# A hybrid decoder block on one core: VectorE's S5 parameters as two interleaved chains, the skip term as a matrix product, and the gates' steps in groups

## The chip, the core and the metric

The kernel runs on one core of a Trainium2 chip. The metric is the device time of one execution in microseconds. The kernel before has a median of 1624.55 us over three runs (1624.2 to 1626.63). The profiled execution took 1620.8 us, of which the trace covers a span of 1618.7 us.

## The reference

The block mixes the sequence (512 tokens, 1024 channels), retrieves experts and adds a gated embedding. Only the mixer's front matters here:

```python
z = rmsnorm(h) @ w_in                    # xs (512), u (512), v (512)
# S5: 32 groups of 16 channels, 64 complex states each
dt = exp(log_dt); mag = exp(lam_re * dt); ang = lam_im * dt
abar = mag * (cos(ang) + 1j * sin(ang))  # discretised transition
coef = (abar - 1) / (lam_re + 1j * lam_im)
bbar = coef * b                          # per group 64 x 16, complex
h[t] = abar * h[t-1] + bbar @ u[t]       # a scan over 512 positions
y = Re(c @ h) + d * u                    # d * u is the skip term
ys = gelu(y); ys = ys * sigmoid(ys @ glu_w + glu_b)      # the gates
yg = gelu(u) * (tril(ws) @ layernorm(gelu(v)) + bs)      # in chunks of 128
h = h + concat(rmsnorm(ys), rmsnorm(yg)) @ w_out
# then PEER: queries, top-k of product keys, gathered experts; a gated embedding; a last norm
```

## The kernel before, in words

The whole program is one function, and the order in which it issues work is the order on every engine's queue: nothing is rescheduled. Each engine works through its own queue in order and waits where an operand is not ready. V is VectorE, S is ScalarE, G is GpSimd (POOL in the profile), PE is TensorE, and loads and stores go through SyncE's queue.

**S5 parameters.** Sixteen pairs of groups stand on 128 partitions, so a parameter is a 128x16 tile (`pt16`). VectorE computes them by polynomials, one small step after another: `exp16` of log_dt (`dt`), then `ldt` and `exp16` again (`mag`), then `ang`, its reduction, sine and cosine (`e1c`, `e1s`), then the powers 1 to 4 of the transition (`pwr`, `pwi`), `rho`, and the coefficients (`co_re`, `co_im`). GpSimd negates `c_pad[:, 1]` into `nci`, copies the powers into `prr` and `pri`, and makes `skip`, which is the identity's last 32 columns times d.

**Blocks of four positions.** Time is cut in 128 steps of L = 4 positions. The 16 pairs are taken in four groups g of four. For each g there are:

- `s5_r(g)`: 12 VectorE products that make the input matrices `rr`, `ri`.
- `s5_par(g)`: TensorE products `ptt` (the kernel within a block of four), transposes of `rr` and `ri` (ScalarE copies them to `w4`).
- `s5_par2(g)`: VectorE adds `skip` to a part of `ptt` in PSUM (L460), then ScalarE copies `ptt` into the triangular `t4` (L461, L464).
- `u4_copy(f)`, `u4_scale(f)`: ScalarE copies of one block of `pz` into `u4` (L530), and VectorE's scaling of it by `x4` (L534).
- `s5_pv(g)`: TensorE products `pv` of `w4` and `u4`; `s5_scan(g)`: VectorE rotates them by tables `rc`, `rs` and scans; `s5_back(g)` rotates back.
- `s5_q(g)`: six VectorE products that make the output matrices `qr`, `nqi`.
- `s5_out(g)`: TensorE products `py`, and ScalarE's GELU into `ysT` (L515).

**Tables.** `rc` and `rs` are 128x16x128 tables of cosines and sines. `table_steps` doubles them seven times on VectorE: six products and sums (`cmul`, L547), and a squaring of nine small steps (`csquare`) between two doublings. It is a generator that is advanced at set places.

**The projections.** `z_mm(cc)` is the xs part of w_in (TensorE, L523, accumulated over four chunks in the four PSUM tiles `pz`). `filler` is a generator of further TensorE work: eight tiles `pj` of the embedding's projection, then v, then u. `fill(n)` advances it by n pieces. A `pj` tile takes one of the four buffers of the pool `psa`, which `pz` holds before.

**The gates.** `ys_split` splits `ysT` into two parts for the products with glu_w; `glu_mm(fo)` makes `pg`; `glu_mix(fo)` applies the sigmoid (`sg`, L709), multiplies (L710), splits the result into `mixh`, `mixl` (L170, L171) and squares it (L714). `norm_v` and `norm_v2` are the statistics and the normalisation of v on VectorE, `wo_split` splits a chunk of w_out on ScalarE and VectorE. Then come `prs` (TensorE, sums of squares, L767), `rss` (L769), `mix_v` (`pm`, L719) and the output projection `po`, whose first product follows the last `pm`.

Of the kernel before, what the change touches and what calls it, by code (L numbers as in the profile page):

```python
# [105 lines left out]
def tile_hybrid_block(ctx: ExitStack, tc: tile.TileContext, x, p_t, cols_d, rows_d, w_in, s5_b, s5_c, glu_w, ws_t,  # L106
# [14 lines left out]
    def col(name, j=0, n=1):  # L121
        o, _ = COLS[name]
        return cols[:, o + j:o + j + n]
# [149 lines left out]


    pq = [P, NPAIR]
    W = V
# [39 lines left out]
    lam_re, lam_im = col("a_re", 0, 16), col("a_im", 0, 16)  # L316
    dt = exp16(col("log_dt", 0, 16), "dt")
    ldt = pt16()
    g_tt(ldt, lam_re, dt, ALU.mult)
    mag = exp16(ldt, "mag")  # L320
    ang = pt16()
    g_tt(ang, lam_im, dt, ALU.mult)
# [24 lines left out]
    cmul(W, e1c, e1s, qc, qs, cr, sr, t1)  # L347


    pwr = sp.tile([P, NPAIR, L], F32, name="pwr")  # L350
# [38 lines left out]
    g_tt(co_im, co_im, den, ALU.mult)  # L389
    nci = sp.tile([P, NPAIR, 32], F32, name="nci")  # L390
    G.tensor_scalar(nci, c_pad[:, 1], -1.0, None, op0=ALU.mult)
    prr, pri = (sp.tile([P, NPAIR, L - 1], F32, name=f"pr{z}") for z in "ri")
# [6 lines left out]
    rhos = sp.tile([P, NPAIR, NJ], F32, name="rhos")  # L399
    rc = sp.tile([P, NPAIR, NJ], F32, name="rc")  # L400
    rs = sp.tile([P, NPAIR, NJ], F32, name="rs")
    G.memset(rc[:, :, 0:1], 1.0)
    G.memset(rs[:, :, 0:1], 0.0)
    for h in range(NF):
# [6 lines left out]
    def s5_r(g, e):  # L411
        g4 = slice(4 * g, 4 * g + 4)
        rr, ri = (fw.tile([P, 4, L, 32], F32, name=f"rr{z}", bufs=2) for z in "ri")
        t3 = fw.tile([P, 4, L - 1, 32], F32, name="t3", bufs=1)
        one = lambda a: a[:, g4, None].to_broadcast([P, 4, 32])
        cmul(e, rr[:, :, 3, :], ri[:, :, 3, :], one(co_re), one(co_im), b_pad[:, 0, g4, :], b_pad[:, 1, g4, :],
             t3[:, :, 0, :])
        shp = [P, 4, L - 1, 32]
        cmul(e, rr[:, :, 0:3, :], ri[:, :, 0:3, :], prr[:, g4, :, None].to_broadcast(shp),
             pri[:, g4, :, None].to_broadcast(shp), rr[:, :, 3:4, :].to_broadcast(shp),  # L420
             ri[:, :, 3:4, :].to_broadcast(shp), t3)
        RR[g] = rr, ri

    def s5_q(g):
        g4 = slice(4 * g, 4 * g + 4)
        qr, nqi = (fw.tile([P, 4, L, 32], F32, name=f"q{z}") for z in "ri")
        tq = fw.tile([P, 4, L, 32], F32, name="tq", bufs=1)
        a_r, a_i = (a[:, g4, :, None].to_broadcast([P, 4, L, 32]) for a in (pwr, pwi))
        c_r, c_i = (a[:, g4, None, :].to_broadcast([P, 4, L, 32]) for a in (c_pad[:, 0], nci))
        V.tensor_tensor(tq, a_i, c_i, op=ALU.mult)  # L430
        V.tensor_tensor(qr, a_r, c_r, op=ALU.mult)
        V.tensor_tensor(qr, qr, tq, op=ALU.add)
        V.tensor_tensor(tq, a_i, c_r, op=ALU.mult)
        V.tensor_tensor(nqi, a_r, c_i, op=ALU.mult)
        V.tensor_tensor(nqi, nqi, tq, op=ALU.subtract)
        QQ[g] = qr, nqi

    def s5_par(g):
# [5 lines left out]
        for q in range(4):  # L444
            o = ptt[:, q * 32:(q + 1) * 32]
            PE.matmul(o, flat(rr[:, q]), c_pad[:, 0, 4 * g + q, :], start=True, stop=False)
            PE.matmul(o, flat(ri[:, q]), nci[:, 4 * g + q, :], start=False, stop=True)
        w4 = [fw.tile([P, 4, P], F32, name=f"w4{z}") for z in "ri"]
        for z, src in enumerate((rr, ri)):
# [3 lines left out]
            S.copy(w4[z].rearrange("p a b -> p (a b)"), pw4)  # L453
        WW[g], TT[g] = w4, (t4, ptt)

    def s5_par2(g):
        t4, ptt = TT[g]
        k3 = ptt[:, 0:P].rearrange("p (q c) -> p q c", q=4)
        k0 = k3[(L - 1) * 32:]
        V.tensor_tensor(k0, k0, skip[(L - 1) * 32:, 4 * g:4 * g + 4, :], op=ALU.add)  # L460
        S.copy(t4[:, :, 3, :], k3)  # L461
        for t in range(3):
            for b in range(t + 1):
                S.copy(t4[32 * b:32 * b + 32, :, t, :], k3[32 * (b + 3 - t):32 * (b + 4 - t)])  # L464
        TT[g] = t4

# [69 lines left out]

    def table_steps():
        sq = csquare(csquare((e1c, e1s)))
        n = 1
        while n < NJ:  # L540
            tt = fw.tile([P, 3 * 4 * NJ], F32, name="tt", tag="sc", bufs=1)[:, 0:NPAIR * NJ // 2].rearrange(
                "p (a j) -> p a j", a=NPAIR)
            ei, er = (a[:, :, None].to_broadcast([P, NPAIR, n]) for a in (sq[1], sq[0]))
            o_re, o_im, b_re, b_im, t_ = rc[:, :, n:2 * n], rs[:, :, n:2 * n], rc[:, :, 0:n], rs[:, :, 0:n], tt[:, :, 0:n]
            for o, a, b, op in ((t_, b_im, ei, ALU.mult), (o_re, b_re, er, ALU.mult), (o_re, o_re, t_, ALU.subtract),
                                (t_, b_im, er, ALU.mult), (o_im, b_re, ei, ALU.mult), (o_im, o_im, t_, ALU.add)):
                V.tensor_tensor(o, a, b, op=op)  # L547
                if 2 * n == NJ:
                    yield
            n *= 2  # L550
            if n in (16, 64):
                yield
            if n < NJ:
                sq = csquare(sq)


    pjd = dpool.tile([NT, P, D], F32, name="pjd")
# [50 lines left out]
    z_mm(0)  # L608
    s5_r(0, V)
    z_mm(1)  # L610
# [5 lines left out]
    G.memset(rhos[:, :, 0:1], 0.0)  # L616
    s5_r(1, V)
    s5_par(0)
    z_mm(2)
    s5_par(1)  # L620
    tab = table_steps()
    next(tab)
    s5_par2(0)
    next(tab)
    s5_par2(1)
    z_mm(3)
    u4_copy(0)
    for n in range(4):
        next(tab)
    u4_scale(0)  # L630
    for n in range(3):
        next(tab, None)
    fill(2)
# [9 lines left out]
    s5_par(2)  # L643
    s5_par2(2)
    u4_scale(2)
# [5 lines left out]
    u4_scale(3)  # L651
    s5_q(0)
    fill(13)
# [10 lines left out]
    s5_back(1, "V")  # L664
    s5_par2(3)
    s5_q(1)
# [39 lines left out]

    def glu_mix(fo, pg):
        sg = rp_.tile([P, T], F32, name="sg", bufs=2)
        S.activation(sg, pg, AF.Sigmoid, bias=col("glu_b", fo))  # L709
        V.tensor_tensor(ysT[fo], ysT[fo], sg, op=ALU.mult)  # L710
        hi, lo = (rp_.tile([P, T], F32R, name=f"mix{z}{fo}") for z in "hl")
        split_scaled(hi, lo, ysT[fo], col("on_ssm", fo))
        mixs.append((hi, lo))
        S.activation(ysT[fo], ysT[fo], AF.Square)  # L714
# [24 lines left out]
    fill(12)  # L739
    for f in range(3):  # L740
        ys_split(f)
    norm_v2(0, *nv[0])
    nv.append(norm_v(1))
    ys_split(3)
    wo_split(0)
    wo_split(1)
    norm_v2(1, *nv[1])
    nv.append(norm_v(2))
    pgs = [glu_mm(fo) for fo in range(NF)]
    fill(8)  # L750
    for fo in range(2):
        glu_mix(fo, pgs[fo])
    norm_v2(2, *nv[2])
    nv.append(norm_v(3))
    for fo in range(2, NF):
        glu_mix(fo, pgs[fo])
    fill(100)
# [635 lines left out]
```

## Time and profile before

| | before |
|---|---|
| median of three runs | 1624.55 us |
| profiled execution | 1620.8 us |
| its span | 1618.7 us |
| mean granted TensorE clock | 0.978 |
| TensorE busy | 1533.8 us (95%) |
| VectorE busy | 1337.1 us (83%) |
| ScalarE busy | 700.5 us (43%) |
| GpSimd busy | 788.9 us (49%) |

The front, which is all that the change touches, ends at about 257 us of the span. The rest is the PEER part. A row of the timeline reads: start, duration, engine, line, operation, output and inputs, count, and in brackets the idle time of that engine ahead of it with what ended it. A row of the chain of waits reads: start, duration, what.

### The profile page before, as it was taken

The numbers are of one execution on the slowest core, as the hardware profiler recorded it, in microseconds if no ns is written. First come the engines' busy times: TensorE is split into PE (matmuls) and PEld (weight loads), VectorE is DVE, ScalarE is ACT, GpSimd is POOL, SyncE is SP. The second block draws the span as 40 slices with busy tenths as digits, with TensorE's granted clock in tenths as the row PEclk, the third lists the DMA queues.
The fourth block names the chain that finished last, engine by engine and source line by source line (L and its number), as shares of the span: only waits on it lengthen the run. The fifth ranks groups of instructions, "written<-read, shape, count | busy, mean of one in ns | idle before, by whom it ended". The sixth has DMA issues, their size and how long they took to land.

```text
span 1618.7 us, 22140 instructions
## 1 busy us (share of the span) xinstructions
PE 1533.8 (95%) x7779; PEld 1334.0 (82%) x7779; DVE 1337.1 (83%) x2688; ACT 700.5 (43%) x1262; POOL 788.9 (49%) x656
## 2 busy tenths in 40 slices
PE   7699698999999898999999999999999999999997
PEld 4355486889998898898888888888888888888886
DVE  8977453789999777769899998998899989989774
ACT  3546323333334888853333333333333333333354
POOL 2000123447887888955455554555545555545201
PEclk9899899999999999999999999999999999999999
DMA  6121113223443454588899998989898999998851
GB/s 242 46 85 52 52 39 130 89 74 115 132 144 109 148 211 186 205 313 314 298 324 332 332 342 307 340 305 349 303 351 303 339 310 330 337 316 328 289 166 66
DMA packets 124431, 366.34 MB, mean 226 GB/s; under 512 B 8736, under 2 KB 60320, under 8 KB 106272
## 3 DMA queue, kind: packets, MB, share of 16 engines
q1 hardware_dynamic: 105888, 230.70, 41.6%
q0 software_dynamic: 18432, 134.23, 22.4%
q8 instruction: 61, 1.00, 0.2%
q14 instruction: 50, 0.41, 0.1%
HBM read 331.47 MB, written 33.42 MB: 225 GB/s over the span
## 4 chain that ended last, share of the span: by engine, by line
PE 60%; DVE 18%; ACT 7%; POOL 5%; issue 5%; DMA 4%; SPq 0%; POOLq 0%; DVEq 0%; ACTq 0%
PE yp L154 9%; PE yp L155 8%; PE yp L153 8%; PE pq L155 7%; PE pq L153 7%; PE pq L154 7%; ACT stg L1095 3%; DMA g<-in_uv,idx 3%; POOL ul L167 3%; PE pgm L1094 2%; PE pz L577 1%; DVE oh L967 1%; DVE oh L964 1%; POOL g L1118 1%; PE pg L154 1%
## 5 line engine op out<-in xcount | busy, mean ns | idle before, releaser
L167 POOL TENSOR_TENSOR ul<-ust,uh 128x256 fp32r<-128x256 f32 (+1 forms) x342 | 430.1, 1284 | 186.2 <-ACT uh L160 186.0
L153 PE MATMUL pq<-hnh,uh 128*128 128x384 f32 (+1 forms) x1152 | 396.7, 344 | 0.8 <-DVE hnl L171 0.8
L155 PE MATMUL pq<-hnh,ul 128*128 128x384 f32 (+1 forms) x1152 | 394.6, 343 | 1.9 <-POOL ul L167 1.9
L154 PE MATMUL pq<-hnl,uh 128*128 128x384 f32 (+1 forms) x1152 | 393.4, 341 | 0.0
L1118 POOL DMA_INDIRECT g<-in_uv,idx x128 | 210.7, 1646 | 314.5 <-DVE y L1161 293.4
L154 PE MATMUL yp<-vl,ah 128*128 128x512 f32 x768 | 301.4, 392 | 4.0 <-DVE vl L162 4.0
L155 PE MATMUL yp<-vh,al 128*128 128x512 f32 x768 | 300.4, 391 | 0.0
L153 PE MATMUL yp<-vh,ah 128*128 128x512 f32 x768 | 298.9, 389 | 0.0
L882 ACT ACTIVATE gab<-pq 128x384 f32<-128x384 f32 x118 | 58.1, 492 | 481.7 <-PE pq L155 481.7
L153 PEld LDWEIGHTS pq<-hnh,uh 128*128 128x128 f32 x1152 | 217.2, 189 | 8.5 <-DVE hnl L171 1.0
L155 PEld LDWEIGHTS pq<-hnh,ul 128*128 128x128 f32 x1152 | 216.6, 188 | 8.9 <-POOL ul L167 3.2
L154 PEld LDWEIGHTS pq<-hnl,uh 128*128 128x128 f32 x1152 | 217.1, 188 | 7.8 <-DVE hnl L171 0.2
L162 DVE TENSOR_TENSOR vl<-vst,vh 128x1024 fp32r<-128x1024 f32 x128 | 161.9, 1265 | 21.9 <-ACT vh L160 21.7
L1150 DVE SCALAR_TENSOR_TENSOR g<-g,hrow 128x1024 f32<-128x1024 f32 x128 | 162.9, 1276 | 20.0 <-DMA g<-in_uv,idx 19.9
L154 PEld LDWEIGHTS yp<-vl,ah 128*128 128x128 f32 x768 | 144.1, 188 | 36.3 <-DVE vl L162 8.0
L155 PEld LDWEIGHTS yp<-vh,al 128*128 128x128 f32 x768 | 144.1, 188 | 29.9
L153 PEld LDWEIGHTS yp<-vh,ah 128*128 128x128 f32 x768 | 144.2, 188 | 28.4
L1161 DVE SCALAR_TENSOR_TENSOR y<-g,act,y 128x1024 f32<-128x1024 f32 x127 | 163.2, 1285 | 4.5
L1154 DVE TENSOR_TENSOR act<-act,gate 128x1 f32<-128x1 f32 (+1 forms) x117 | 156.6, 1338 | 0.0
L160 ACT CAST uh<-ust 128x1024 fp32r<-128x1024 f32 x144 | 150.9, 1048 | 0.1
L160 ACT CAST vh<-vst 128x1024 fp32r<-128x1024 f32 x128 | 134.2, 1049 | 1.2 <-DMA vst<-in_uv 1.0
L1077 POOL TENSOR_SCALAR o1P<-iota,tr 128x128 f32<-128x128 f32 x96 | 112.0, 1178 | 3.6 <-ACT tr L1034 3.6
(412 smaller groups left out, 2117.4 us busy)
## 6 DMA issues: line engine op xcount, KB each, us to landing
ust<-in_ut SPq DMA_DIRECT2D x128, 512.0 KB, 7.5
vst<-in_uv SPq DMA_DIRECT2D x128, 512.0 KB, 6.3
gd<-stg SPq DMA_DIRECT2D x12, 2048.0 KB, 7.2
gread<-gd SPq DMA_DIRECT2D x31, 768.0 KB, 8.3
ust<-in_wq SPq DMA_DIRECT2D x16, 512.0 KB, 3.4
wstage<-in_w_in SPq DMA_DIRECT2D x12, 512.0 KB, 7.8
wstage<-in_w_out SPq DMA_DIRECT2D x8, 512.0 KB, 3.5
ust<-in_ple_wg SPq DMA_DIRECT2D x8, 512.0 KB, 6.9
```

The costliest lines, as they stand in the source:

```text
L153: PE.matmul(o, lh, rh, start=start, stop=False)
L154: PE.matmul(o, lh, rl, start=False, stop=False)
L155: PE.matmul(o, ll, rh, start=False, stop=stop)
L160: S.copy(hi, src)
L162: V.tensor_tensor(lo, src, hi.bitcast(F32), op=ALU.subtract)
L167: G.tensor_tensor(l[:, sl], s[:, sl], h[:, sl], op=ALU.subtract)
L882: S.activation(ga[n], p_[:, 0:TD], AF.Gelu)
L1077: (V if e == "V" else G).tensor_scalar(o1[a], iota, i1, g, op0=ALU.is_equal, op1=ALU.mult)
L1118: G.indirect_dma_start(out=gt, out_offset=None, in_=uv, in_offset=bass.IndirectOffsetOnAxis(ap=idx[:, r:r + 1], axis=0))
L1150: V.scalar_tensor_tensor(GS[k][:, 0:D], GS[k][:, 0:D], 1.0, hrow0, op0=ALU.mult, op1=ALU.mult, accum_out=dots[:, k:k + 1])
L1154: V.tensor_tensor(act[:, k:k + n], act[:, k:k + n], gates[0][:, k:k + n], op=ALU.mult)
L1161: V.scalar_tensor_tensor(y0, t[:, D:], act[:, k:k + 1], y0, op0=ALU.mult, op1=ALU.add)
```

## The change

- A class `Later` collects VectorE's instructions instead of issuing them, and `play(a, b)` issues one of the list a, then one of the list b, until a is empty. The chain of `ldt` and `mag` goes into list `ca`, that of `ang` to `e1c`, `e1s` into `cb`; they are issued in turns. Then the powers and coefficients go into `ca` and the whole table (`tables`) into `cb`, again in turns.
- `s5_r(0)`, `s5_r(1)` and `s5_q(0)` go into `ca` and are issued in turns with further table steps; `s5_q(0)` stood behind `u4_scale(3)` before. What is left of the table is issued behind `z_mm(3)`, with `u4_scale(0)` ahead of its last two steps.
- The skip term is a third product into `ptt` (`ident` times `skip`), so that VectorE's addition in `s5_par2` goes; the ScalarE copies into `t4` are issued at the end of `s5_par`.
- `nci` is no tile of its own: `c_pad[:, 1]` is negated in place. The tile `t3` gets two buffers.
- `ys_split` of all four follows `norm_v2(0)` and `norm_v(1)`; `fill(8)`, which stood ahead of the first `glu_mix`, goes, and its pieces are issued by `fill(100)` behind the last one.
- `glu_mix` is cut in two: `glu_gate` (sigmoid and product) for all four, then `norm_v(3)`, then `glu_mix` (split and square) for all four. `sg` gets three buffers.

```diff
+    class Later:
+        def __init__(self):
+            self.ops = []
+        def __getattr__(self, name):
+            return lambda *a, **k: self.ops.append((name, a, k))
+        def play(self, n):
+            for name, a, k in self.ops[:n]:
+                getattr(V, name)(*a, **k)
+            del self.ops[:n]
+
+    def play(a, b, upto=0):
+        while len(a.ops) > upto:
+            a.play(1)
+            b.play(1)
...
     dt = exp16(col("log_dt", 0, 16), "dt")
+    ca, cb = Later(), Later()
+    W = ca
     ldt = pt16()
     g_tt(ldt, lam_re, dt, ALU.mult)
     mag = exp16(ldt, "mag")
+    W = cb
     ang = pt16()
...
     cmul(W, e1c, e1s, qc, qs, cr, sr, t1)
+    play(ca, cb)
+    cb.play(len(cb.ops))
+    W = ca
...
-    nci = sp.tile([P, NPAIR, 32], F32, name="nci")
-    G.tensor_scalar(nci, c_pad[:, 1], -1.0, None, op0=ALU.mult)
+    rc = sp.tile([P, NPAIR, NJ], F32, name="rc")
+    rs = sp.tile([P, NPAIR, NJ], F32, name="rs")
+    G.memset(rc[:, :, 0:1], 1.0)
+    G.memset(rs[:, :, 0:1], 0.0)
+
+    def tables(e):
+        tt = fw.tile([P, 3 * 4 * NJ], F32, name="tt", tag="sc", bufs=1)[:, 0:NPAIR * NJ // 2].rearrange(
+            "p (a j) -> p a j", a=NPAIR)
+        sq = csquare(csquare((e1c, e1s)))
+        n = 1
+        while n < NJ:
+            cmul(e, rc[:, :, n:2 * n], rs[:, :, n:2 * n], rc[:, :, 0:n], rs[:, :, 0:n],
+                 *(a[:, :, None].to_broadcast([P, NPAIR, n]) for a in sq), tt[:, :, 0:n])
+            n *= 2
+            if n < NJ:
+                sq = csquare(sq)
+
+    W = cb
+    tables(cb)
+    play(ca, cb)
+    nci = c_pad[:, 1]
+    G.tensor_scalar(nci, nci, -1.0, None, op0=ALU.mult)
...
-            PE.matmul(o, flat(ri[:, q]), nci[:, 4 * g + q, :], start=False, stop=True)
+            PE.matmul(o, flat(ri[:, q]), nci[:, 4 * g + q, :], start=False, stop=False)
+            PE.matmul(o, ident, skip[:, 4 * g + q, :], start=False, stop=True)
...
-        WW[g], TT[g] = w4, (t4, ptt)
-
-    def s5_par2(g):
-        t4, ptt = TT[g]
         k3 = ptt[:, 0:P].rearrange("p (q c) -> p q c", q=4)
-        k0 = k3[(L - 1) * 32:]
-        V.tensor_tensor(k0, k0, skip[(L - 1) * 32:, 4 * g:4 * g + 4, :], op=ALU.add)
         S.copy(t4[:, :, 3, :], k3)
...
     z_mm(0)
-    s5_r(0, V)
+    s5_r(0, ca)
+    play(ca, cb)
     z_mm(1)
...
-    s5_r(1, V)
     s5_par(0)
+    s5_r(1, ca)
+    s5_q(0, ca)
+    play(ca, cb)
     z_mm(2)
     s5_par(1)
-    tab = table_steps()
-    next(tab)
-    s5_par2(0)
-    next(tab)
-    s5_par2(1)
     z_mm(3)
     u4_copy(0)
-    for n in range(4):
-        next(tab)
+    cb.play(len(cb.ops) - 2)
     u4_scale(0)
-    for n in range(3):
-        next(tab, None)
+    cb.play(2)
     fill(2)
...
-    s5_q(0)
     fill(13)
...
-    def glu_mix(fo, pg):
-        sg = rp_.tile([P, T], F32, name="sg", bufs=2)
+    def glu_gate(fo, pg):
+        sg = rp_.tile([P, T], F32, name="sg", bufs=3)
         S.activation(sg, pg, AF.Sigmoid, bias=col("glu_b", fo))
         V.tensor_tensor(ysT[fo], ysT[fo], sg, op=ALU.mult)
+
+    def glu_mix(fo):
...
     fill(12)
-    for f in range(3):
-        ys_split(f)
     norm_v2(0, *nv[0])
     nv.append(norm_v(1))
-    ys_split(3)
-    wo_split(0)
-    wo_split(1)
+    for f in range(NF):
+        ys_split(f)
     norm_v2(1, *nv[1])
     nv.append(norm_v(2))
+    wo_split(0)
     pgs = [glu_mm(fo) for fo in range(NF)]
-    fill(8)
-    for fo in range(2):
-        glu_mix(fo, pgs[fo])
+    wo_split(1)
     norm_v2(2, *nv[2])
+    for fo in range(NF):
+        glu_gate(fo, pgs[fo])
     nv.append(norm_v(3))
-    for fo in range(2, NF):
-        glu_mix(fo, pgs[fo])
+    for fo in range(NF):
+        glu_mix(fo)
     fill(100)
```

More of the change, by code (lines that the diff above doesn't have):

```diff
@@ L399, in tile_hybrid_block @@
     rhos = sp.tile([P, NPAIR, NJ], F32, name="rhos")
[L400 to L403, printed above, removed]
     for h in range(NF):
@@ L413, in s5_r @@
         rr, ri = (fw.tile([P, 4, L, 32], F32, name=f"rr{z}", bufs=2) for z in "ri")
-        t3 = fw.tile([P, 4, L - 1, 32], F32, name="t3", bufs=1)
+        t3 = fw.tile([P, 4, L - 1, 32], F32, name="t3")
         one = lambda a: a[:, g4, None].to_broadcast([P, 4, 32])
@@ L422, in s5_r, with s5_q @@
         RR[g] = rr, ri
-    def s5_q(g):
+    def s5_q(g, V=V):
         g4 = slice(4 * g, 4 * g + 4)
@@ L464, in s5_par2 @@
                 S.copy(t4[32 * b:32 * b + 32, :, t, :], k3[32 * (b + 3 - t):32 * (b + 4 - t)])
-        TT[g] = t4
+        WW[g], TT[g] = w4, t4
     def s5_pv(g):
@@ L534, in u4_scale @@
         V.tensor_tensor(uf, uf, x4[:, None, :].to_broadcast([P, 4, NJ]), op=ALU.mult)
[L537 to L554, printed above, removed]
     pjd = dpool.tile([NT, P, D], F32, name="pjd")
@@ L643, in tile_hybrid_block @@
     s5_par(2)
-    s5_par2(2)
     u4_scale(2)
@@ L664, in tile_hybrid_block @@
     s5_back(1, "V")
-    s5_par2(3)
     s5_q(1)
```

## The prediction

> **What bounds the kernel now.** I read the times first, then the busy time of each engine by stage, then the timeline of one engine at a time in the stages that the edits touch, and last the chain of waits around the gates. The first fence is the page's first line and the busy time by stretch (PE, PEld, VectorE, ScalarE, GpSimd, then the granted clock).
>
> ```profile
> span 1618.7 us, 22140 instructions
> 49.10:61.59 12.49, 0.00 (x0) 0.00 (x1) 11.92 (x31) 5.93 (x23) 0.00 (x0) 0.68 0.13 43
> 181.30:196.78 15.48, 1.56 (x7) 1.29 (x6) 8.86 (x22) 7.17 (x12) 1.55 (x2) 0.67 0.11 34
> 260.00:1618.00 1358.00, 1322.64 (x6944) 1192.94 (x6944) 1154.72 (x2209) 589.62 (x1005) 757.17 (x584) 0.99 0.72 253
> ```
>
> From 260 us on TensorE is busy 1322.6 of 1358 us: the PEER part is bound by it, the diff doesn't touch it, and it should only begin earlier. What can be won lies ahead of it, where TensorE once stands still for 12.5 us and once works 1.6 us in 15.5. The next rows show who is late in the first of these: VectorE's front in order of time, then TensorE's and ScalarE's.
>
> ```profile
> 6.30 0.17 DVE L290 TENSOR_TENSOR s5p<-cols,dt 128x16 f32<-128x16 f32 x1
> 9.94 0.18 DVE L290 TENSOR_TENSOR mag<-eq,eni 128x16 f32<-128x16 f32 x1
> 10.03 0.17 DVE L290 TENSOR_TENSOR s5p<-cols,dt 128x16 f32<-128x16 f32 x1
> 13.50 0.81 DVE L339 SCALAR_TENSOR_TENSOR s5p<-s5p,s5p 128x16 f32<-128x16 f32 x4
> 16.48 0.18 DVE L290 TENSOR_TENSOR pwr<-mag,s5p 128x16 f32<-128x16 f32 x1
> 23.15 0.29 DVE L187 TENSOR_TENSOR t<-s5p,b_pad 128x128 f32<-128x128 f32 x1
> 28.33 0.29 DVE L187 TENSOR_TENSOR t<-s5p,b_pad 128x128 f32<-128x128 f32 x1
> 33.23 0.25 DVE L290 TENSOR_TENSOR s5p<-s5p 128x16 f32<-128x16 f32 x2
> 44.09 0.29 DVE L547 TENSOR_TENSOR rc<-rc,tt 128x128 f32<-128x128 f32 x1
> 45.27 0.32 DVE L460 TENSOR_TENSOR ptt<-ptt,skip 32x128 f32<-32x128 f32 x1
> 61.57 0.69 DVE L534 TENSOR_TENSOR u<-u,x 128x512 f32<-128x512 f32 x1
> 62.18 1.22 DVE L547 TENSOR_TENSOR rs<-rc,s5p 128x1024 f32<-128x1024 f32 x1
> 64.57 0.29 DVE L187 TENSOR_TENSOR t<-s5p,b_pad 128x128 f32<-128x128 f32 x1
> 88.86 0.68 DVE L430 TENSOR_TENSOR tq<-pwi,nci 128x512 f32<-128x512 f32 x1
> ```
>
> ```profile
> 28.44 0.38 PE L447 MATMUL ptt<-nci,rri 128*128 128x32 f32 x2 [1.41 <-POOL t L442]
> 42.04 7.03 PE L523 MATMUL pz<-xn,wstage 128*128 128x512 f32 x16
> 61.59 3.78 PE L564 MATMUL pj<-gu,ysT 128*128 128x512 f32 x4 [12.52 <-ACT u L530]
> 70.98 1.16 PE L472 MATMUL pv<-u,w4r 128*128 128x128 f32 x8 [1.20 <-DVE u L534]
> 94.69 0.38 PE L510 MATMUL py<-u,t 128*128 128x128 f32 x2
> 55.35 0.27 ACT L461 COPY t<-ptt 128x128 f32<-128x128 f32 x1 [7.79 <-DVE ptt L460]
> 57.25 4.28 ACT L530 COPY u<-pz 32x128 f32<-32x128 f32 x16
> ```
>
> TensorE's product `pj` at 61.59 needs a buffer that `pz` holds until `u4_copy(0)` has read it. That copy (57.25) stands on ScalarE behind the second copy of `ptt` (55.35), which waits 7.8 us for VectorE's addition of `skip`, and VectorE is in the middle of the table. So VectorE's chain of small steps sets the front up to the scans, and TensorE waits for it. The second gap is at the gates: first VectorE and TensorE, then the chain of waits, then what follows it.
>
> ```profile
> 156.12 1.89 DVE L162 TENSOR_TENSOR ysl<-ysT,ysh 128x512 fp32r<-128x512 f32 x3 [8.07 <-ACT ysh L160]
> 162.74 0.50 PE L154 MATMUL pg<-ysl,wglu2h 128*128 128x512 f32 x1 [1.10 <-DVE ysl L162]
> 171.71 9.60 PE L577 MATMUL pz<-wstage,xn 128*128 128x512 f32 x22
> 179.90 0.70 ACT sg L709
> 180.62 0.70 DVE ysT L710
> 181.35 0.73 ACT mixh L170
> 182.10 0.76 DVE mixl L171
> 182.89 0.63 ACT ysT L714
> 186.36 1.04 DVE gv L603 x4
> 190.44 0.59 DVE ysT L710
> 196.78 5.71 PE prs L767 x26
> 196.75 1.28 ACT L579 ACT_TABLE_LOAD   x1
> 199.20 1.04 ACT L160 CAST wo2h<-wstage 128x1024 fp32r<-128x1024 f32 x1
> 205.03 0.16 DVE L769 COPY rss<-prs 128x8 f32<-128x8 f32 x1
> 208.18 0.47 PE L153 MATMUL po<-wo0h,mixh 128*128 128x512 f32 x1
> ```
>
> There ScalarE and VectorE hand each other one tile at a time, with the sigmoid, the product, both parts of the split and the square in one string for each of four tiles, from 179.9 to 196.8 us. TensorE's `prs` waits for the last square.
>
> **The change part by part: the front.** *Two chains in turns.* A step of 128x16 that needs the one before starts about 0.21 us after it (the 19 steps from 6.30 to 10.03 take 0.20 each); one that doesn't starts 0.09 us after it (9.94 to 10.03). The `mag` chain has 19 steps and the `ang` chain 33, so each pair takes about 0.21 us: 19 pairs are 4.0 us, from 6.30 to 10.3, and the last 14 steps take what they take now, 13.7 (the second of the four at 13.50) to 16.48, 2.8 us at most. The powers start at about 12.8 instead of 16.48: 3.7 us won. Then 35 steps of powers and coefficients, now 16.48 to 23.15, run in turns with 35 table steps, each pair again 0.21: 7.4 us, with an allowance of 0.8 us for GpSimd's negation and `skip`, which touch the same memory in that stretch: `s5_r(0)` begins at about 20.9 instead of 23.15. Without the allowance it is 20.1; if pairs cost twice as much, it is later than before, which is the second rival.
>
> *`s5_r` and `s5_q(0)` in turns with 30 table steps.* `s5_r(0)` is 5.2 us (23.15 to 28.33), `s5_r(1)` 4.9 (28.33 to 33.23), `s5_q(0)` 4.0 (88.86 to the next step, six of 0.69 that overlap a little). A small step in the gap of a large dependent one costs nothing and elsewhere 0.09; I take 0.04 each, 1.2 us for 30. So `s5_r(0)` ends at 26.5, `s5_r(1)` at 31.9, `s5_q(0)` at 36.3. By then 65 of the 114 table steps are done. The other 49 lie now between 44.09 and the end of the table at 64.57: 20.5 us, less two additions of `skip` (0.7) and `u4_scale(0)` (0.6), 19.2 us. So `u4_scale(0)`, ahead of the last two steps of 1.2 each, stands at 36.3 + 16.8 = 53.1 instead of 61.57, and the table ends at 56.1 instead of 64.57: 8.5 us earlier.
>
> *The skip term on TensorE.* Four products more in each `s5_par`. A pair of records of that shape takes 0.38 us and overlaps the next, so 0.9 us a group, 1.5 at most. For the groups 0 and 1 it is on TensorE's path: `ptt` goes on with `rri` at 26.5 instead of 28.44, then what takes 13.6 us today (28.44 to 42.04) takes 15.4, and `z_mm(3)` starts at 41.9 and ends at 48.9, as now. Its first tile is ready a quarter into it, ScalarE is past its copies of `ptt` at about 44.4 because they wait for no addition, and `u4_copy(0)` (4.3 us) ends at 48.7. TensorE's `pj` then starts at 48.9 instead of 61.59. What is late next is VectorE: `s5_pv(0)` waits for `u4_scale(0)` until 53.8, and `s5_pv(1)`, behind `s5_r(2)` on VectorE, starts at about 61.9 instead of 70.98, 9.0 us earlier (a little over VectorE's 8.5, since `u4_copy(1)` is no longer late).
>
> From there to `s5_out(0)` TensorE has 23.7 us of work today (70.98 to 94.69), plus 0.9 for the third skip product, less some 0.7 of waits for late copies: 8.8 us are left. `s5_q(0)`'s 4.0 us leave VectorE at 88.86, where TensorE's `fill(13)` is the longer, so that gives nothing more. In group 3 the product hides behind VectorE's scan and the addition of 0.3 leaves VectorE's path. The front gives 9 us. Its bounds: 6 if every small step and every skip product costs its upper value, 11 if TensorE's warm stretch also shortens `fill(13)` (the 12.5 us gap had the clock at 0.68).
>
> *What moves at no cost.* The two memsets of `rc`, `rs` go ahead of the negation on GpSimd, which is idle there; without that cover the table's first product would wait for `c_pad`. Negating in place is the same instruction. ScalarE's copies into `t4` come earlier and wait only for `ptt`. `s5_q(0)` issues six VectorE products and no DMA; SyncE's queue is passed by nothing in the front.
>
> **The gates.** VectorE is idle 8.1 us ahead of `ysl` (156.12), so `norm_v2(0)` and `norm_v(1)`, 4.1 us (as from 186.36 to 190.44), now fit in that gap; the fourth `ysl` comes at once, and TensorE's 1.1 us wait at 162.74 goes. In the times of today, with the front's gain set aside, the four `pg` end at 170.6 (171.71 less 1.1). VectorE has by then nearly done what stands ahead of the gates: from 158.5 on one and a half times those 4.1 us and two `wo_split`, each a little over the 1.04 of ScalarE's part, some 9 us. Four sigmoids follow the `pg` as they come, since the u pieces' GELUs and the table's reload stand behind them now. After the last `pg`: sigmoid 0.70, product 0.70, `norm_v(3)` 1.6 (of the 4.1): 173.6. The first `mixh` is done in that time. Then four strings of `mixl` 0.76, square 0.63 and `mixh` 0.73, without sigmoid and product: 2.15 us each with the handing over, the last square at 181.5 instead of 196.7. This is 15.2 us.
>
> What is late next: `prs` at 181.5 (the u products, moved past nothing on TensorE, end at 180.2, from 171.71 + 9.60 - 1.1), but ScalarE must first reload its table and do four GELUs where two stood: 196.75 to 199.20 is 2.45, two more are 1.3, so `wo2h` is at 185.2. From `wo2h` to `rss` it is 5.8 us now (199.20 to 205.03), hence 191.1; the last `pm` waits for `rss`' buffer, and `po` follows after eight records, which is 0.9 to 1.8 us (`prs` takes 0.22 a record behind its wait, half of that warm), or 3.2 as today (205.03 to 208.18). I take 1.4, as TensorE has nothing else left by then: `po` at 192.5 instead of 208.18, 15.7 us. The bounds are 12.5 (3.2 for the last step, and a string of mixes that takes 0.35 us more each) and 17 (ScalarE not last). The last two loads of w_out keep waiting for the u products on SyncE's queue, which end 1.1 us earlier, and are wanted seven us later; a DMA is not late here.
>
> **The sum.** 9.0 + 15.7 = 24.7 us off the span of 1618.7: 1594.0, and the profiled execution 1596.1 instead of 1620.8. The median shown is 3.75 us above that execution, so 1599.8; I say 1600.
>
> **A rule against it.** Against the first part stands VectorE's pipeline. The Trainium skill, "VectorE: DVE Perf Modes", section "The DRAIN you can't avoid", says that the next operation doesn't start before the pipe has emptied and that leaving out the semaphore doesn't avoid it; by that rule two chains in turns take the sum of both, and the result is the second rival's 1611. The same section grants that an operation that isn't held starts earlier, and the trace sides with that half: the step at 10.03, which needs nothing of the one at 9.94, starts within the latter's 0.18 us.
>
> **The rivals.** *Only the front, or little of the gates, pays.* If ScalarE or VectorE find a new order at the gates that ends as late as now (the GELUs of u hold back all of w_out's splits), what is left is 9 + 1.1: 1614.5. For it: ScalarE's GELUs and the reload stand behind all four mixes. Against it: the mixes lose eight hand-overs.
>
> *Turns hide nothing.* If each small step costs its 0.21 whatever stands between, the 35 table steps come as 5.5 us ahead of `s5_r(0)` (today 33.23 on) and 30 more as 5.3 us among the large ones. Then `s5_r(0)` ends at 36, `z_mm(3)` at 58, the scans start 2.7 us later than now, and the front loses 2.5 us: 1624.5 + 2.5 - 15.7 = 1611. The rows at 9.94 and 10.03 speak against it.
>
> *Slower, by the clock.* The gaps go, and TensorE works more densely. If the clock that is granted in the PEER part, 0.99 over 1358 us, fell for that, each hundredth would cost 13.7 us; the change would come out slower from 0.97 on, and 1630 at 0.968. Against it: the low clocks stand in the gaps (0.68 and 0.67), and the dense 1358 us have 0.99.
>
> **How the numbers follow.** Both parts as worked out: 0.82, by itself 1594.5 to 1606 (front 6 to 11, gates 12.5 to 17, and a microsecond or two for the runs' own spread). Gates or front failing: 0.07 each, 1614.5 and 1611. Slower by the clock or another thing: 0.02, no change 0.02. The range goes from 1593.5 to 1611.5, so that it takes in the second rival. 0.2% (3.2 us) is about what a measurement can tell from no change. Faster 0.95, same 0.02, slower 0.03.
>
> **What would show it.** Right: small VectorE steps of the front start every 0.1 us; `s5_r(0)` starts near 21; TensorE's `pj` starts near 49 and `s5_out(0)` near 86; no VectorE additions on `ptt`; the last gate square lies 15 to 16 us closer to the end of `glu_mm`; `po` starts near 183 and the PEER part keeps its length. Wrong: pairs spaced 0.4 us apart; TensorE idle between the last u product and `po` for over 10 us; a longer PEER part, or its clock below 0.99.

## The result, and the profile after

The changed kernel takes 1597.67 us (median of four runs, 1595.83 to 1600.21) where the kernel before took 1624.38 in the same comparison: a ratio of 0.9839, interval 0.9815 to 0.9863. The profiled execution took 1596.47 us, its span is 1594.2; the prediction said 1600, 1596.1 and 1594.0. The same program in a second comparison gave 1601.79; what lies between the two is taken up with the experiments.

The page's first line of the changed kernel:

```profile
span 1594.2 us, 22196 instructions
```

Its busy time by stretch (TensorE, its weight loads, VectorE, ScalarE, GpSimd, then the granted clock and DMA), from the first gate product `pg` to `po`, and the PEER part from its first query product:

```profile
150.61:183.50 32.89, 30.16 (x137) 22.16 (x135) 21.27 (x48) 19.25 (x25) 5.44 (x5) 0.95 0.21 65
244.28:1594.20 1349.92, 1316.35 (x6913) 1187.22 (x6913) 1152.21 (x2205) 587.90 (x1003) 755.94 (x583) 0.99 0.72 253
```

The same two stretches of the kernel before:

```profile
158.74:208.18 49.44, 34.41 (x137) 25.79 (x135) 27.26 (x63) 19.49 (x25) 7.97 (x8) 0.79 0.14 43
267.56:1618.70 1351.14, 1316.94 (x6913) 1187.77 (x6913) 1151.77 (x2205) 588.09 (x1003) 756.24 (x583) 0.99 0.72 253
```

From `pg` to `po` it is 32.9 us instead of 49.4: 16.6 us. TensorE stood still for 15.0 us of the stretch and now for 2.7, and the same 137 products take 30.2 instead of 34.4 us, at a granted clock of 0.95 instead of 0.79. What lies ahead of it, here called the front, gives 8.1 us (`pg` at 150.61 instead of 158.74). The PEER part, counted from its first query product `pq` on, has 6913 products in both and is as long as before to within 1.2 us. Before, it begins at 267.56; the output projection and what follows it fill the 59 us from `po` to there.

The front in order of time. VectorE first (start, duration, line, operation):

```profile
6.20 0.26 DVE L285 TENSOR_TENSOR s5p<-cols,dt 128x16 f32<-128x16 f32 x2
6.41 0.17 DVE L285 TENSOR_SCALAR ex<-s5p 128x16 f32<-128x16 f32 x1
6.50 0.18 DVE L285 TENSOR_SCALAR s5p<-s5p 128x16 f32<-128x16 f32 x1
6.62 0.17 DVE L285 TENSOR_SCALAR en<-ex 128x16 f32<-128x16 f32 x1
9.92 0.17 DVE L285 TENSOR_TENSOR mag<-eq,eni 128x16 f32<-128x16 f32 x1
12.74 0.18 DVE L285 TENSOR_TENSOR pwr<-mag,s5p 128x16 f32<-128x16 f32 x1
14.69 0.60 DVE L285 TENSOR_TENSOR s5p<-s5p 128x16 f32<-128x16 f32 x1
17.04 1.07 DVE L285 TENSOR_TENSOR s5p<-s5p,s5p 128x16 f32<-128x16 f32 x1
21.56 0.29 DVE L285 TENSOR_TENSOR t<-s5p,b_pad 128x128 f32<-128x128 f32 x1
53.81 0.68 DVE L570 TENSOR_TENSOR u<-u,x 128x512 f32<-128x512 f32 x1
```

Then GpSimd, ScalarE and TensorE in the same stretch:

```profile
14.64 1.52 POOL L436 TENSOR_SCALAR c_pad<-c_pad 128x512 f32<-128x512 f32 x1 [2.54 <-DMA c_pad<-in_s_c]
17.04 1.03 POOL L442 TENSOR_TENSOR skip<-ident,cols 128x512 f32<-128x512 f32 x1
45.33 4.29 ACT L566 COPY u<-pz 32x128 f32<-32x128 f32 x16
31.19 8.15 PE L559 MATMUL pz<-xn,wstage 128*128 128x512 f32 x16
49.67 1.98 PE L580 MATMUL pj<-gu,ysT 128*128 128x512 f32 x4
62.43 1.16 PE L508 MATMUL pv<-u,w4r 128*128 128x128 f32 x8 [1.12 <-DVE u L570]
```

A step of one chain starts within the step of the other: `ex` at 6.41, the other chain's at 6.50, `en` at 6.62. The last step of the `mag` chain starts at 9.92, where it started at 9.94 before, and the 19th step of the other chain right behind it, at 10.02. ScalarE's copy of block 0 (45.33) no longer stands behind a copy that waits for VectorE, and the product `pj` starts at 49.67 instead of 61.59.

The gates, on ScalarE, VectorE and TensorE in turn:

```profile
154.01 0.69 ACT L718 ACTIVATE sg<-pg,cols 128x512 f32<-128x512 f32 x1 [1.22 <-PE pg L155]
162.41 0.69 ACT L718 ACTIVATE sg<-pg,cols 128x512 f32<-128x512 f32 x1 [2.11 <-PE pg L155]
166.10 0.63 ACT L725 ACTIVATE ysT<-ysT 128x512 f32<-128x512 f32 x1 [2.39 <-DVE mixl L171]
172.29 0.63 ACT L725 ACTIVATE ysT<-ysT 128x512 f32<-128x512 f32 x1 [0.82 <-DVE mixl L171]
176.52 1.06 ACT L160 CAST wo2h<-wstage 128x1024 fp32r<-128x1024 f32 x1
182.37 0.16 DVE L778 COPY rss<-prs 128x8 f32<-128x8 f32 x1
182.59 1.16 PE L730 MATMUL pm<-gv,wsm 128*128 128x128 f32 x8 [2.14 <-DVE rss L778]
183.50 0.67 PE L153 MATMUL po<-wo0h,mixh 128*128 128x512 f32 x1
```

Each sigmoid waits for nothing but its own `pg` (every 2.8 us), the last square is at 172.29 instead of 196.1, and `po` at 183.50 instead of 208.18. The last `pm` still waits 2.14 us for `rss`.

### The profile page after: what moved, and what is told of

The parts are those of the page before. It is cut to its first block, busy times and chain, and to the rows that moved or that the text cites. A ratio compares the mean times of both kernels' runs of the same rounds, so it can differ in the third digit from the quotient of the medians.

```text
span 1594.2 us, 22196 instructions
## 1 busy us (share of the span) xinstructions
PE 1533.3 (96%) x7811; PEld 1334.0 (84%) x7811; DVE 1328.4 (83%) x2684; ACT 699.9 (44%) x1262; POOL 788.9 (49%) x656
## 4 chain that ended last, share of the span: by engine, by line
PE 61%; DVE 20%; ACT 6%; POOL 5%; issue 5%; DMA 3%; POOLq 0%; DVEq 0%; ACTq 0%
PE yp L154 9%; PE yp L155 9%; PE yp L153 9%; PE pq L155 7%; PE pq L153 7%; PE pq L154 7%; ACT stg L1104 3%; DMA g<-in_uv,idx 3%; POOL ul L167 3%; PE pz L593 2%; PE pgm L1103 2%; DVE oh L976 1%; DVE oh L973 1%; PE pg L153 1%; PE pg L155 1%
```

## The experiments

Runs of one program spread by some microseconds, so the starts of marked instructions in each trace carry more than the times. All are from the timelines, in us: `r0` is the first step of `s5_r(0)`, `pv1` the first product of `s5_pv(1)`, `py` that of `s5_out(0)`, `sq` the last gate square, `pq` the first PEER product; PEER is the span's end less `pq`.

| kernel | r0 | pj | pv1 | py | pg | sq | po | pq | PEER | time, ratio (interval) |
|---|---|---|---|---|---|---|---|---|---|---|
| before | 23.15 | 61.59 | 70.98 | 94.7 | 158.7 | 196.1 | 208.2 | 267.6 | 1351.1 | |
| after | 21.56 | 49.67 | 62.43 | 87.0 | 150.6 | 172.3 | 183.5 | 244.3 | 1349.9 | 1597.67, 0.9839 (0.9815 to 0.9863) |
| after_again | 21.47 | 47.77 | 62.4 | 86.9 | 150.5 | 172.2 | 183.4 | 243.5 | 1354.6 | 1601.79, 0.9873 (0.9851 to 0.9896) |
| front_only | 21.47 | 49.5 | 62.35 | 87.0 | 150.5 | 187.9 | 200.7 | 260.4 | 1358.3 | 1613.92, 0.9937 (0.9915 to 0.996) |
| gates_only | 23.00 | 61.42 | 70.81 | 96.0 | 160.1 | 181.8 | 193.0 | 253.1 | 1353.5 | 1607.99, 0.9893 (0.9867 to 0.9919) |
| no_turns | 28.66 | 59.49 | 72.84 | 97.4 | 161.0 | 182.7 | 193.9 | 254.8 | 1353.4 | 1611.09, 0.9919 (0.9895 to 0.9944) |
| fill8_back | 21.65 | 49.7 | 62.54 | 87.1 | 150.7 | 182.2 | 194.6 | 254.2 | 1352.5 | 1610.63, 0.9919 (0.9891 to 0.9947) |
| string_gates | 21.68 | 49.7 | 62.60 | 87.2 | 150.8 | 176.5 | 188.3 | 247.6 | 1355.4 | 1605.35, 0.9872 (0.985 to 0.9895) |
| skip_vec | 21.54 | 50.84 | 63.13 | 88.3 | 152.4 | 174.0 | 185.3 | 246.2 | 1356.2 | 1604.88, 0.9881 (0.9866 to 0.9896) |
| q_late | 21.30 | 50.97 | 59.59 | 85.7 | 149.3 | 171.0 | 182.2 | 243.0 | 1349.5 | 1599.78, 0.9852 (0.9837 to 0.9868) |
| best | 21.46 | 47.79 | 59.2 | 86.5 | 150.1 | 165.7 | 181.4 | 241.1 | 1355.4 | 1598.45, 0.983 (0.9808 to 0.9853) |
| best2 | 21.55 | 49.54 | 59.3 | 86.1 | 149.7 | 165.3 | 181.1 | 240.5 | 1353.7 | 1595.81, 0.9821 (0.9799 to 0.9843) |

**The two halves apart.** *front_only* has the new front and the old gates, *gates_only* the reverse.

```diff
 front_only
...
-    wo_split(1)
+    fill(8)
+    for fo in range(2):
+        glu_mix(fo, pgs[fo])
     norm_v2(2, *nv[2])
-    for fo in range(NF):
-        glu_gate(fo, pgs[fo])
     nv.append(norm_v(3))
-    for fo in range(NF):
-        glu_mix(fo)
+    for fo in range(2, NF):
+        glu_mix(fo, pgs[fo])
```

> The changed front with the gates of before. Theory (two gains that add, one behind the other): the trace of the changed kernel has the first output product of the last group 8.1 us earlier, so the time is 1624.4 - 8.1 = 1616.3 us, span about 1610.6. Rival (the gates alone decide, the front's gain is only waited away there): 1624 us, no change.

> The changed gates with the front of before. Theory: the rest of the 24.5 us of the two spans, 16.4 us: 1608 us, span about 1602.3. Rival (the gates gain only because the front feeds them earlier): 1620 us or more.

Alone, the front brings `po` 7.5 us earlier and the gates 15.2; together they bring it 24.7, 2 us more than the sum. The times lie 9.7 and 15.6 us below the 1623.58 of the kernel before in that comparison. Expected were 1616.3 and 1608; measured are 1613.92 and 1607.99. So both parts pay, and neither needs the other; the rivals, in which one of them gives little, fall. The profiled execution of front_only was the slowest of its five (1620.92) and its span, 1618.7, is no shorter than before: its PEER part is 7.2 us longer, which hides the 7.5 us at `po`.

**The turns.** Each list is issued as a whole, so that the same instructions stand one chain behind the other.

```diff
     def play(a, b, upto=0):
-        while len(a.ops) > upto:
-            a.play(1)
-            b.play(1)
+        n = len(a.ops) - upto
+        a.play(n)
+        b.play(n)
```

> The changed kernel with the same VectorE steps at the same places, but each list issued whole, first a, then as many of b, instead of in turns. Theory (turns hide the 0.1 us that a dependent small step waits): the 35 table steps come as 5.5 us behind the coefficients and 30 more as 5.3 us among the large products, less some 2 us that turns cost anyway, and the first pair of chains loses 3.7 us; the scans start 9 to 11 us later than in the changed kernel, and the time is 1597.7 + 9 to 11, 1607 to 1609 us. Rival (a pair of lists takes the sum of both either way, and the gain of the front comes from ScalarE's copies that no longer wait for the addition of skip): within 2 us of 1597.7.

VectorE in that kernel, the end of the `mag` chain and the first product of `s5_r(0)`:

```profile
9.61 0.17 DVE L285 CAST eni<-en 128x16 int32<-128x16 f32 x1
9.82 0.17 DVE L285 TENSOR_TENSOR mag<-eq,eni 128x16 f32<-128x16 f32 x1
9.91 0.17 DVE L285 TENSOR_TENSOR s5p<-cols,dt 128x16 f32<-128x16 f32 x1
28.66 0.28 DVE L285 TENSOR_TENSOR t<-s5p,b_pad 128x128 f32<-128x128 f32 x1
```

A dependent step starts 0.21 us behind its forerunner (9.61 to 9.82), one of another chain 0.09 (9.82 to 9.91). `s5_r(0)` starts 7.1 us later than with turns, the scans and `po` 10.4 later, and by `py` the front is 2.7 us behind the kernel before. The rival, within 2 us of 1597.7, falls. So all of the front's gain hangs on the turns: with everything else in place, and above all with 35 table steps moved ahead of `s5_r(0)` and 30 more among the products behind it, the front is slower than before. What the other edits would give without turns and with the table where it stood was not run. The 10.4 us lie within the expected 9 to 11; the time, 1611.09, is 2 us above the expected 1607 to 1609, and in the profiles the PEER part is 3.5 us longer than after the change.

**What the gates gain by.** *fill8_back* puts the u pieces back ahead of the sigmoids and keeps the grouping; *string_gates* leaves them where the change puts them and has the strings of before.

```diff
 fill8_back
+    fill(8)
     for fo in range(NF):
         glu_gate(fo, pgs[fo])
 string_gates (the front of the change, the gates of before without this line)
-    fill(8)
```

> The changed kernel with the eight u pieces issued ahead of the gates again, as before. Theory (what counts at the gates is that the sigmoids no longer stand on ScalarE behind two GELUs that wait for the u products; the grouping is the smaller part): the first sigmoid starts about 8 us behind the last gate product again, the last square comes some 11 us later than in the changed kernel, 1597.7 + 9 to 12, about 1608 us. Rival (the grouping of the four gates is what gains): within 4 us of 1597.7.

> The changed front, and the gates of before (one string of steps for each tile, two tiles, then two norms, then two tiles) with only the eight u pieces taken away from ahead of them. Theory (ScalarE's GELUs ahead of the sigmoids were most of the loss): the first sigmoid starts within 2 us of the first gate product's end or when VectorE has done the norms, a tile takes 3.5 us, the last square comes some 4 us later than in the changed kernel, po starts at about 187.5 instead of 183.5, time about 1601.7 us. Rival (without the grouping nothing is won): po at 197 or later, 1611 us.

ScalarE, first in front_only (the old gates), then in fill8_back, then in string_gates:

```profile
169.73 0.69 ACT L595 ACTIVATE gu<-pz,xr 128x512 f32<-128x512 f32 x1 [1.03 <-PE pz L593]
...
171.72 0.69 ACT L718 ACTIVATE sg<-pg,cols 128x512 f32<-128x512 f32 x1
```

```profile
166.83 0.69 ACT L595 ACTIVATE gu<-pz,xr 128x512 f32<-128x512 f32 x1 [15.23 <-PE pz L593]
170.53 2.42 ACT L718 ACTIVATE sg<-pg,cols 128x512 f32<-128x512 f32 x4
```

```profile
155.56 0.69 ACT L718 ACTIVATE sg<-pg,cols 128x512 f32<-128x512 f32 x1 [2.65 <-PE pg L155]
161.71 0.72 ACT L170 ACTIVATE mixh<-ysT,cols 128x512 fp32r<-128x512 f32 x1 [5.45 <-DVE ysT L719]
176.46 0.63 ACT L723 ACTIVATE ysT<-ysT 128x512 f32<-128x512 f32 x1 [0.82 <-DVE mixl L171]
```

In fill8_back ScalarE waits 15.2 us for the u product that stands ahead of the sigmoids in its queue. After the change the first sigmoid could start at 154.0 and the last at 162.4; here all four come from 170.5 on, and `po` is 11.1 us later. Taking the pieces away from the old strings (front_only to string_gates) gives 12.3 us, and the rest of the gates' edits, what is left from string_gates to after, 4.8. In the other order it is 6.0 (front_only to fill8_back) and 11.1. So about two thirds of these 17 us are the wait in ScalarE's in-order queue, which the prediction hadn't separated. The smaller part is not the grouping alone: string_gates also has the old places of `ys_split`, `wo_split` and the two norms, and from its second square to its third (166.76 to 172.96) it takes 6.2 us where the others follow after 3.5. How much of the 4.8 is hand-overs and how much these places was not taken apart. Both theories were right in the points (`po` of string_gates 188.3 where 187.5 was expected), and both rivals fall: fill8_back isn't within 4 us of after, and string_gates has `po` long before 197. Both times are above what was expected, 1610.63 for about 1608 and 1605.35 for 1601.7, with PEER parts 2.6 and 5.5 us longer than after the change.

**The skip term on VectorE again.** The third product goes, the addition comes back, with the table's steps ahead of it.

```diff
-            PE.matmul(o, ident, skip[:, 4 * g + q, :], start=False, stop=True)
...
+        V.tensor_tensor(k0, k0, skip[(L - 1) * 32:, 4 * g:4 * g + 4, :], op=ALU.add)
```

> The changed kernel with the skip term added by VectorE again instead of a third product; for the groups 0 and 1 the additions stand in the middle of the table, 19 steps behind s5_q(0), where ptt is ready. Theory (what counts is where the addition stands, not which engine does it): VectorE has 0.7 us more ahead of u4_scale(0), TensorE 0.9 us less in each s5_par; the scans and the first output product within 1 us of the changed kernel's (62.4 and 87.0), time 1597.7 within 1 us. Rival (an addition on VectorE holds up ScalarE's copies and with them pj, as before): pj at 55 or later, 3 us or more lost.

TensorE's products of the second block in skip_vec, and VectorE's third addition:

```profile
63.13 2.08 PE L513 MATMUL pv<-u,w4r 128*128 128x128 f32 x8 [2.46 <-DVE u L575]
70.14 0.32 DVE L501 TENSOR_TENSOR ptt<-ptt,skip 32x128 f32<-32x128 f32 x1 [0.88 <-PE ptt L488]
```

A narrow miss in the points, and the clock is in it. The scans start 0.7 us later (63.13), as the 0.7 us of VectorE's additions say, and `py` 1.3 us later, not within 1. Between the two TensorE saves the third product's 0.9 us, but it loses 1.5 at the products `pv`, which take 2.08 us instead of 1.16 (those of the other half 1.68 instead of 1.06) at a granted clock of 0.53. ScalarE's copies do wait for the additions, as in the rival, and `pj` is 1.2 us later at 50.84, far from the rival's 55. So `po` is 1.8 us later in this profile, but without those 1.5 us the two forms would be about level: which one is better isn't shown. The time, 1604.88, lies 7.2 us above after's, and 6.3 of that are in the PEER part, which this edit doesn't touch. The last control below has 4.7 us of such a difference in one and the same program; whether all of the 6.3 is of that kind isn't shown either.

**`s5_q(0)` behind the scaling again.** With it out of the turns, the table is done earlier.

```diff
     s5_r(1, ca)
-    s5_q(0, ca)
     play(ca, cb)
...
     u4_scale(3)
+    s5_q(0)
     fill(13)
```

> The changed kernel with s5_q(0) back behind u4_scale(3), as before. Theory (its six products are 3.6 us of VectorE's time ahead of u4_scale(0), which TensorE waits for, while VectorE has 12.9 us of idle time behind s5_r(3)): the scans start 3.5 us earlier, at about 59, the first output product at about 84, and the time is 1597.7 - 3, about 1594.7 us. Rival (ScalarE's copies of u or TensorE's own work set these times, or the wait moves behind s5_back(0)): the first output product within 1 us of 87.0.

TensorE where the second block of scans begins in q_late, and the busy time and clock from there to 63.00:

```profile
59.59 2.07 PE L508 MATMUL pv<-u,w4r 128*128 128x128 f32 x8 [3.13 <-DVE u L570]
```

```profile
59.59:63.00 3.41, 3.41 (x17) 3.41 (x18) 3.34 (x6) 2.85 (x12) 0.00 (x0) 0.53 0.10 40
```

The scans are 2.8 us earlier, but `py` only 1.3 and `po` the same 1.3: TensorE had waited 3.13 us, and its first products then ran at a granted clock of 0.53, the eight shown in 2.07 us instead of 1.16, the next eight in 1.70 instead of 1.06. That is the 1.5 us by which the way from `pv1` to `py` is longer, 26.1 us instead of 24.6. After the change the low clock falls ahead of `pv1`, and from there to `py` the clock is 1.00. The expectation of 1594.7 was too low by 5, and the rival (`py` within 1 us of 87.0) isn't met either; 1599.78 is not to be told from after.

**Two steps on.** *best* takes q_late and gives the gates as a pipeline: three sigmoids and products, then splits (`mix_h`) and squares (`mix_s`) with the fourth gate in between, the last `norm_v` behind them. *best2* also moves two splits of w_out and the last norm's second half ahead of the last `fill`; those are the last three added lines and the three taken out below. The edit of q_late and the halves of `glu_mix` aren't shown.

```diff
-    for fo in range(NF):
+    for fo in range(3):
         glu_gate(fo, pgs[fo])
-    nv.append(norm_v(3))
-    for fo in range(NF):
-        glu_mix(fo)
+    mix_h(0)
+    mix_h(1)
+    glu_gate(3, pgs[3])
+    mix_s(0)
+    mix_h(2)
+    mix_s(1)
+    mix_h(3)
+    mix_s(2)
+    mix_s(3)
+    nv.append(norm_v(3))
+    wo_split(2)
+    norm_v2(3, *nv[3])
+    wo_split(3)
     fill(100)
...
-    wo_split(2)
-    norm_v2(3, *nv[3])
-    wo_split(3)
```

> As the run before (s5_q(0) late), and at the gates the mixes issued in a pipeline: the first two splits ahead of the fourth gate, each square one tile behind its split, norm_v(3) behind the squares. Theory (a string of split and square is 2.1 us by hand-overs, while ScalarE alone needs 1.3): the last square comes at 167 less 3, before TensorE's u products end, so that ScalarE's GELUs and wo2h come 4 us earlier; po starts about 7.5 us earlier than 183.5, and TensorE isn't cold there, which is 1.4 us; time about 1589 us, span 1585. Rival (TensorE's u products or the GELUs end as late, and nothing but the first part is won): 1594.7 us.

> This is the kernel with Wq's first block behind all of u's scaling and the gates in a pipeline, with the block means' weights and norms (the splits of Wo of 2 and 3, the third norm) moved ahead of the last fill of products, so that TensorE and VectorE have less to do between the last square and the first product with Wo. Theory (the chain from the last square over the last GELUs and Wo's casts to rss sets the first product): po at about 179.5 (183.50 after the change, 181.44 without the move), time about 1593. Rival (TensorE at half clock behind its waits, and the PEER part's low stretches, which fall anew in each execution, take what the points gain): po no earlier than 181, time within 2 us of after's.

TensorE in best2 from its first sums of squares on, in order of time, and behind it the busy time by stretch:

```profile
170.76 4.53 PE L786 MATMUL prs<-ones,ysT 128*128 128x2 f32 x32
175.15 6.17 PE L733 MATMUL pm<-gv,wsm 128*128 128x128 f32 x32
181.08 0.47 PE L153 MATMUL po<-wo0h,mixh 128*128 128x512 f32 x1
```

```profile
149.72:181.08 31.36, 31.36 (x137) 23.71 (x135) 25.88 (x56) 19.06 (x25) 8.77 (x6) 0.89 0.21 68
174.00:180.00 6.00, 6.00 (x30) 6.00 (x30) 4.67 (x6) 1.42 (x2) 3.60 (x2) 0.50 0.00 0
```

The squares end 7 us earlier than after the change and the first cast of `wo2h` is at 165.9 instead of 176.5, as the theory wants, yet `po` comes only 2.4 us earlier, at 181.1. The chain over the last square no longer sets it: `rss` is there at 175.33, 5.7 us ahead of `po`. TensorE has no gap in the whole stretch from `pg` to `po`, 31.36 of 31.36 us, but a granted clock of 0.50 from 174 to 180. So the theory of best2 (179.5) misses, and the rival's number (no earlier than 181) holds; its half clock is there too, but not behind a wait, as it had said. Once TensorE is the bound, what other engines save doesn't move `po`. best misses more clearly: `po` at 181.4 where 176 was expected, 0.8 us earlier than in q_late, and 1598.45 us where 1589 was expected, not to be told from after or from best2. Against after_again, which ran beside it, best2's runs are 6 us lower (1591.13 to 1597.08 against 1600.06 to 1604.11) and the two intervals of the ratio don't overlap; in the profiles `po` is 2.3 us earlier, `pq` 3.0 and the PEER part 0.9 shorter. Against the changed kernel's first comparison (1597.67) it is 1.9 us lower, and the intervals overlap. So best2 is ahead by 2.3 us at `po` for reasons that are shown; that its time is lower by more than that isn't.

**The changed kernel once more.** Unchanged.

> The changed kernel once more, unchanged, as the measure of what one profile differs from another by. Theory (up to the first PEER product the points belong to the kernel, behind it the low stretches belong to the execution): the points up to po within 0.5 us of the first profile (u4_scale 53.8, pv(1) 62.4, first block of y 87.0, gates 150.6, po 183.5), the PEER part anywhere from 1349 to 1358, time 1597.7 within 2. Rival (the low stretches belong to the kernel too): the PEER part within 1 us of 1349.9.

TensorE in after_again:

```profile
30.44 7.03 PE L559 MATMUL pz<-xn,wstage 128*128 128x512 f32 x16
47.77 1.99 PE L580 MATMUL pj<-gu,ysT 128*128 128x512 f32 x4
182.48 1.16 PE L730 MATMUL pm<-gv,wsm 128*128 128x128 f32 x8 [0.51 <-DVE rss L778]
```

The points that VectorE or ScalarE set repeat to 0.1 us (`pv1` 62.4, `py` 86.9, `po` 183.4); those that TensorE sets by itself move with the clock, as `pj` does by 1.9 us. The PEER part is 4.7 us longer, and with it the time 4.1 us higher, not within the expected 2: the rival, a PEER part within 1 us of the first, falls. What of the 4.7 us belongs to the execution and what to the chip isn't known, since the two comparisons may have run on different chips.

## Why the prediction was right

**The turns (front, first step): right.** Powers at 12.8 (12.74 measured); `s5_r(0)` near 20.9 came at 21.56. What was sized too small is the allowance for GpSimd, 0.8 us: two steps of VectorE took 0.60 and 1.07 us instead of 0.18, at the very times of GpSimd's negation (14.64) and `skip` (17.04), together 1.3 us longer. That is 0.5 of the 0.7 us by which `s5_r(0)` is late. The size could have been read from the kernel before, where the steps at these two operations (14.90 and 19.88 there) are as slow:

```profile
14.92 0.63 DVE L345 SCALAR_TENSOR_TENSOR s5p<-s5p,s5p 128x16 f32<-128x16 f32 x1
19.99 0.97 DVE L192 TENSOR_TENSOR pwi<-pwi,s5p 128x16 f32<-128x16 f32 x1
```

**The front's later points: 0.5 to 1 us late each, as they hang on that.** `u4_scale(0)` 53.1 predicted, 53.81 measured; `pj` 48.9 and 49.67; `s5_pv(1)` 61.9 and 62.43; `py` 86 and 87.04. From `s5_pv(1)` to `py` it is 24.61 us against 23.71 before: the skip product's 0.9 us was right (the products into `ptt` take from 66.04 to 68.64, where they took from 74.58 to 76.29), and the 0.7 us of late copies that the prediction took off didn't go: TensorE waits 0.73 us for `w4r` in both. At `pg` the front gives 8.1 us, not 9.0. The bounds, 6 to 11, hold.

**The gates: right, a little low.** Counted from the first `pg`, the prediction has the last square's end 22.8 us later, `wo2h` 26.5, `rss` 32.4, `po` 33.8; measured were 22.3, 25.9, 31.8 and 32.9. The strings take 2.06 us each (166.10 to 172.29 for three) where 2.15 was taken, and from `rss` to `po` it is 1.1 us instead of 1.4. So it is 16.6 us instead of 15.7: the front's error and this one cancel, and that the sum at `po` is 24.7 as predicted is an accident.

**The rest shifted whole: not quite.** Behind `po` the prediction moved everything by the same amount, but the first query product came 23.3 us earlier, not 24.7. From `po` to there it takes 60.8 us instead of 59.4, at a granted clock of 0.92 instead of 0.94: there is one stretch of half clock more, and it stands right behind `po`. The changed kernel there, and then the kernel before:

```profile
183.50:187.30 3.80, 3.80 (x13) 3.01 (x12) 3.80 (x6) 0.00 (x0) 2.71 (x2) 0.55 0.00 0
```

```profile
208.18:212.00 3.82, 3.82 (x20) 3.15 (x19) 3.82 (x12) 0.82 (x3) 1.01 (x3) 1.00 0.00 0
```

The kernel before has 20 products there, the change 13. This goes with the new gates and not with one execution: in the six profiles that have them as the change does (after, after_again, gates_only, no_turns, skip_vec, q_late) it is 60.1 to 61.0 us from `po` to `pq`, at 0.91 or 0.92; in the other six it is 59.3 to 59.7, at 0.94. What in the gates brings it isn't shown. A wait stands ahead of `po`, 2.14 us in after, but in after_again it is 0.51 and the extra half clock comes later, ahead of `pq`. The PEER part then came out 1.2 us shorter, and the span's gain is 24.7 - 1.4 + 1.2 = 24.5 us. Neither term was in the prediction; that they nearly cancelled is luck, since the second is within what two executions of one program differ by.

**The rivals.** That the gates don't pay falls by gates_only. That turns hide nothing falls by no_turns, and with it the rule that was set against the change: the Trainium skill's sentence ("VectorE: DVE Perf Modes", "The DRAIN you can't avoid") that the next operation doesn't start before the pipe has emptied holds here for a step of the same chain, 0.21 us, and not for one of the other, 0.09. That rival's price was good in its parts, `py` 2.7 us later than before for its 2.5; that the time without turns is the same too, 1611 and 1611.09, is in part chance, as the PEER part was 2.3 us longer there than before. That the PEER clock falls is refuted at its size, 0.99 in both; but the sentence that supported this, that the low clocks stand in the gaps, was too simple, as the last section shows.

## What to carry to other kernels

A chain of small dependent steps left more than half of VectorE free here (0.21 us against 0.09 from step to step): look for a second chain that is needed soon and issue the two in turns, and check that nothing else uses their memory in that time. On an in-order queue a wait for work of another engine holds back everything behind it, and that (11 to 12 us here) is worth looking for before the order of the tiles themselves (5 to 6 us). Once the engine that is the bound has no gap left, as TensorE in the gates of best2, count its own products and its clock before anything else is moved.

## What the runs showed of the hardware

In all twelve traces the granted clock is 1.0 or 0.5, in stretches of 3.41 us or a multiple. They fall on a grid that differs between executions of one kernel: `z_mm(2)` took 8.15 us in the first profile (31.19), with half clock up to 33.4, and 7.03 in the second, with none there. The Trainium skill, "TensorE: Matmul & The Clock Gate", Part 1, has such a window of about 3.4 us that runs free of the kernel and halves the clock after an idle one; the grid and the half agree. Not agreeing is that it takes an idle window: in best2 it was half for 6 us without idle time of TensorE in the records, during the 128x2 sums of squares and the `pm` products. It can't be told here what in them counts as idle.

In the PEER part such stretches begin at nearly the same places of every trace, about 250, 274, 298, 322, 360, 381 and 418 us behind `pq`, but which of them occur differs. Here the same 240 us of the span, in the change and in its repetition:

```profile
490.00:730.00 240.00, 220.70 (x1419) 207.95 (x1420) 176.34 (x372) 179.36 (x307) 185.99 (x173) 0.98 0.59 214
```

```profile
490.00:730.00 240.00, 220.56 (x1403) 208.16 (x1404) 173.18 (x370) 179.31 (x306) 181.72 (x171) 0.96 0.58 211
```

In all twelve profiles the PEER part is 1349.5 to 1358.3 us, with 10.2 to 27.3 us at half clock in its first 1000. The shortest (q_late, after) have the least and the longest (front_only) the most; in between the order is loose, with 20.5 us in parts from 1352.5 to 1356.2 us long, so that something else is in the spread too. Two medians of the changed kernel differ by 4 us, about what 10 us more at half clock make (10.2 in after's profile, 20.5 in after_again's), and that is why effects under some 5 us were read here from the start of an instruction, not from the time.
